# Zero products ahead of the first projection, the first weight tile between the halves of x, and one multiply from POOL to DVE

## The chip, the core and the metric

The kernel runs on one core of one Trainium2 chip. The core has five engines with a queue of instructions each: PE (TensorE, the matrix products; a product is a load of the stationary operand, shown as PEld, and a matmul), DVE (VectorE), ACT (ScalarE), POOL (GpSimd) and SP, which here only starts transfers. The metric is the device time of one execution in microseconds, the median of several runs. Beside it stands a profile of one execution: every instruction with its start, its duration and what ended the idle time of its engine before it. Times in the profile count from the first instruction.

## The reference

One layer of a streaming encoder, for x of 1024 tokens by 1024 channels, in float32. Three sub-layers, each normalised before and after and added to x:

```
h    = rms_norm(x, mix_pre_g);  proj = h @ w_in          # u, q, k, v, f_logit
y    = concat(rms_norm(s5_mixer(u)), rms_norm(forgetting_attention(q, k, v, f_logit)))
x    = x + rms_norm(y @ w_out)
x    = x + rms_norm(memory_cross_attention(rms_norm(x), rms_norm(mem)))
x    = x + rms_norm(swiglu(rms_norm(x), w_gate, w_up, w_down))
```

The parts that matter here are the very first product, u = h @ w_in[:, :512], and the very last steps: the down product of the SwiGLU, its norm with the gain `ffn_post_g`, and the addition of x.

## The kernel before

Every float32 product is made of three products of split operands. `split` (L112) makes the high part of an operand on ACT (a copy into a rounded type, L113, scaled by a gain where one is given) and the low part on DVE (the source less the high part, L115, or L117 with a gain). `mm3` (L121) then does high by high (L122), high by low (L123) and low by high (L124) into one bank of PSUM.

**The front.** The traced program begins with small constants and the first step of the generator `ssm()`, which prepares the tables of the state-space branch on DVE. Then, at a raised priority (L913), comes the projection of u. It runs over eight tiles k of 128 channels. For each k, x's transposed tile of 128x1024 is fetched (`x_fetch`, L201) and split with the gain `g_mix` (`x_split`, L207); the weight tile of 128x512 is fetched and split (`u_load`, L260); and `u_part` (L267) does 24 products, three for each of eight blocks of 128 tokens, into eight banks of 512 columns that add up over k. The first four banks come from the pool `g`, the other four are halves of two tiles of the pool `s`. For k = 0, x is fetched and split in two halves of 512 columns, and both are traced ahead of the weight. `x_square` (L212) adds up the squares of x on ACT and DVE for the norm; the norm's factor is applied to u afterwards (`u_scale`, L281).

Weights wait in two `raw` buffers and their split parts in three `whl` buffers, so a later weight can be split only when PE is done with an earlier one. After the last k, `u_keep` (L271) empties the banks; the state-space work then goes on, on DVE for the most part, between the other projections (`in_proj`, L885), the attention heads (`fox`, L705), the cross-attention and the SwiGLU.

**The end.** The down product is put together from seven groups of products. `take` (L1481) treats each bank as it comes. In the last group (n = 4) for each of four blocks j of 128 tokens it adds the bank to a kept sum on DVE (L1479), squares the result on ACT with a sum along the row (`square`, L1468) and multiplies it with the gain on POOL (L1476), in place, so the multiply waits for the square. `finish` (L1505) turns the two sums of squares into the factor r (`rsqrt_mean`, L126: L135 to L145 on DVE, L137 and L138 on ACT), and L1514 multiplies by r and adds x for each half row. For the last block, (t, j) = (1, 3), each half is stored as soon as it is done (L1517).

**What sets the order.** The program is traced in the order in which the Python runs. A planner then puts the instructions of each engine, and the transfers that SP starts, into a fixed order: it walks through a simulated time and takes among what is ready the instruction of the highest priority, the earlier traced one first (`schedule_with_timeline_sim=True`, L1603). On the chip each engine keeps that order and waits where an operand isn't there. A change in one place can therefore move instructions elsewhere.

Of the kernel before, what the change touches and what calls it, by code (L numbers as in the profile page):

```python
# [11 lines left out]
BF16 = mybir.dt.bfloat16  # L12
AF = mybir.ActivationFunctionType
ALU = mybir.AluOpType
# [3 lines left out]
P = 128  # L18
# [21 lines left out]
HID = ("11", "12", "22", "S1", "S2", "S3", "S4")  # L40
EVB = 13
OPB = 10


def bc(ap, axis, n):
# [7 lines left out]
def layer(ctx: ExitStack, tc: tile.TileContext, a, out):  # L53
    nc = tc.nc
    dve, act, pool, pe, sp = nc.vector, nc.scalar, nc.gpsimd, nc.tensor, nc.sync
# [13 lines left out]
    def slab(shape, dt=F32R):  # L69
        return slabp.tile(shape, dt, name="slab", tag="slab")  # L70

    def whl(shape, dt=F32R):
        return whlp.tile(shape, dt, name="whl", tag="whl")

    def raw(shape):
        return rawp.tile(shape, F32, name="raw", tag="raw")

    def g_ps(shape):
        return psg.tile(shape, F32, name="g", tag="g")

    def s_ps(shape):
        return pss.tile(shape, F32, name="s", tag="s")
# [20 lines left out]
    g_mix, g_xa, g_mem, g_out, g_pre_ffn = (gains[:, i, :] for i in range(5))  # L103
# [8 lines left out]
    def split(hi, lo, src, mul=None, lo_eng=None):  # L112
        first = act.activation(out=hi, in_=src, func=AF.Copy, scale=1.0 if mul is None else mul)  # L113
        if mul is None:
            (lo_eng or dve).tensor_tensor(out=lo, in0=src, in1=hi.bitcast(F32), op=ALU.subtract)  # L115
        else:
            dve.scalar_tensor_tensor(out=lo, in0=src, scalar=mul, in1=hi.bitcast(F32),  # L117
                                     op0=ALU.mult, op1=ALU.subtract)
        return first
# [75 lines left out]
    def tt(tag, shape=None, dt=F32):  # L195
        return t4.tile(shape or [P, S], dt, name=tag, tag=tag, bufs=BUFS[tag])
# [4 lines left out]
    def x_fetch(xts, k, n=1):  # L201
        x2t = slab([P, 2, S], F32) if k % 2 == 0 else xts[-1][0]
        xts.append((x2t, x2t[:, k % 2]))
        for cs in (slice(i * S // n, (i + 1) * S // n) for i in range(n)):
            sp.dma_start(out=xts[k][1][:, cs], in_=a["xT"][k * P:(k + 1) * P, cs])

    def x_split(xts, xs, k, n=1):  # L207
        for cs in (slice(i * S // n, (i + 1) * S // n) for i in range(n)):
            hi = split(xs[0][k][:, cs], xs[1][k][:, cs], xts[k][1][:, cs], g_mix[:, k:k + 1])
        return hi  # L210

    def x_square(xts, acc, k):  # L212
        if k == 0:
            act.activation(out=acc, in_=xts[k][1], func=AF.Square)
        else:
            sq = tt("b")
            act.activation(out=sq, in_=xts[k][1], func=AF.Square)
            dve.tensor_tensor(out=acc, in0=acc, in1=sq, op=ALU.add)
# [5 lines left out]
    def x_stats(acc):  # L224

        r = const.tile([P, L], F32, name="r_x")
        ps = s_ps([P, L])
        for j in range(L):
            pe.matmul(ps[:, j:j + 1], acc[:, j * P:(j + 1) * P], ones[:, 0:1], start=True, stop=True)
        rsqrt_mean(r, ps, D)  # L230
        return r, row_bcast(r, L)
# [28 lines left out]
    def u_load(k):  # L260
        w = raw([P, 512])
        sp.dma_start(out=w, in_=a["w_u"][k])
        hl = whl([P, 2, 512])
        split(hl[:, 0], hl[:, 1], w)
        return hl

    def u_part(banks, k, w, xh, xl):  # L267
        for j, ps in enumerate(banks):
            mm3(ps, xh[:, j * P:(j + 1) * P], xl[:, j * P:(j + 1) * P], w[:, 0], w[:, 1], k == 0, k == KT - 1)

    def u_keep(us, banks):  # L271

        for j, ps in enumerate(banks):
            p = ps.rearrange("c (g i) -> c g i", i=16)
            act.activation(out=us[0][:, :, L - 1 - j], in_=p[:, 0:16], func=AF.Copy)
            done = dve.tensor_copy(us[1][:, :, L - 1 - j], p[:, 16:32])
            if j == 3:
                last = done
        return us, last

    def u_scale(us, r):  # L281
        for j in range(L):
            a_, b_ = (u[:, :, L - 1 - j] for u in us)
            act.activation(out=a_, in_=a_, func=AF.Copy, scale=r[:, j:j + 1])
            dve.tensor_scalar(out=b_, in0=b_, scalar1=r[:, j:j + 1], scalar2=None, op0=ALU.mult)

    def qk_tile(i, xH, xL, rb, ahead=False):
        o = tt("a")

        def evac(h, hs, ps):  # L290
            dve.scalar_tensor_tensor(out=by_chunk(o)[:, 4 * h:4 * h + 4], in0=ps.rearrange("p (j c) -> p j c", j=4),
                                     scalar=-0.125 if i < 4 else 1.0,
                                     in1=rb[0][:, hs].rearrange("p (j c) -> p j c", j=4), op0=ALU.mult, op1=ALU.mult)
        yield from proj_tile(load_w(a["w_f"][i], P), xH, xL, evac, ahead)
        stA.dma_start(out=qk_d[i], in_=o)
# [572 lines left out]
    def step(g, n=1):  # L868
        for _ in range(n):
            if next(g, "end") == "end":  # L870
                return
# [40 lines left out]
    step(gs)  # L912
    with tc.high_priority(offset=boost):  # L913
        xts = []
        x_fetch(xts, 0, 2)
        xs = [[slab([P, 2, S]) for _ in range(KT // 2)] for _ in range(2)]
        xH, xL = ([x[k // 2][:, k % 2] for k in range(KT)] for x in xs)
        acc_x = tt("d")
        banks = [g_ps([P, 512]) for _ in range(4)]
        banks += [b[:, h * 512:h * 512 + 512] for b in (s_ps([P, S]) for _ in range(2)) for h in range(2)]  # L920
        ws = [u_load(0)]
        x_split(xts, (xH, xL), 0, 2)
        u_part(banks, 0, ws[0], xH[0], xL[0])
        for k in range(1, KT):
            x_fetch(xts, k)
            ws.append(u_load(k))
            x_split(xts, (xH, xL), k)
            u_part(banks, k, ws[k], xH[k], xL[k])
            x_square(xts, acc_x, k - 1)
        x_square(xts, acc_x, KT - 1)  # L930
        us = [slab([P, 16, L, 16], F32) for _ in range(2)]
        for t in us:
            dve.memset(t[:, 0, 0, 0:1], 0.0)
        u_c, kept = u_keep(us, banks)
        step(gs)
        with tc.issue_after(kept.ins):
            step(gs, 2)
        rb = []
        k4 = qk_tile(4, xH, xL, rb, ahead=True)
        step(k4)  # L940
        r_x, row = x_stats(acc_x)
        rb.append(row)
        u_scale(u_c, r_x)
# [91 lines left out]
    for j in range(NT):  # L1035
# [3 lines left out]
        t = tt("aab"[j % 3])  # L1039
# [3 lines left out]
        for h in range(2):  # L1043
            hs = slice(h * 512, h * 512 + 512)
# [26 lines left out]
    xT, xr, pts, x1_read = {}, {}, {}, []  # L1071
# [290 lines left out]
    tile_pool = lambda name, bufs: fst.enter_context(tc.tile_pool(name=name, bufs=bufs, reuse_waits="tile"))  # L1362
    evp, ssp, opp, wtp = (tile_pool("evp", EVB), tile_pool("ssp", 3), tile_pool("opp", OPB), tile_pool("wtp", 1))
    hid, made = {}, [None]
# [82 lines left out]
    g_fq = gp_.tile([P, D], F32, name="g_fq")  # L1447
# [18 lines left out]
    LO, HI = slice(0, 512), slice(512, 1024)  # L1466

    def square(t, j, h, src):  # L1468
        sq = bp.tile([P, 512], F32, name="sq", tag="sq")
        act.activation(out=sq, in_=src, func=AF.Square, accum_out=ssq[:, t, j, h:h + 1])  # L1470

    def quarter(t, j, hs):

        c = acc[t][j][:, hs]
        square(t, j, 0 if hs is LO else 1, c)
        pool.tensor_tensor(out=c, in0=c, in1=g_fq[:, hs], op=ALU.mult)  # L1476

    def add(o, ps, t):
        dve.tensor_tensor(out=o, in0=ps, in1=t, op=ALU.add)  # L1479
# [1 line left out]
    def take(n, j, ps):  # L1481

        e, o = acc[0][j], acc[1][j]
        if n == 1:
            act.activation(out=e[:, HI], in_=ps, func=AF.Copy)
        elif n == 6:
            add(o[:, LO], ps, e[:, HI])
        elif n == 2:
            square(0, j, 0, ps)
            dve.tensor_tensor(out=e[:, LO], in0=ps, in1=g_fq[:, LO], op=ALU.mult)  # L1490
        elif n == 5:
            add(e[:, HI], ps, e[:, HI])
        elif n == 7:
            add(o[:, HI], ps, e[:, HI])
            quarter(1, j, HI)
        elif n == 3:
            add(e[:, HI], ps, e[:, HI])
            quarter(0, j, HI)
            finish(0, j)
        else:  # L1500
            add(o[:, LO], ps, o[:, LO])
            quarter(1, j, LO)
            finish(1, j)
# [20 lines left out]
    banks = {}  # L1524
# [82 lines left out]
```

## Time and profile before

| | |
|---|---|
| time, median of 3 runs (lowest to highest) | 1432.68 us (1431.65 to 1433.4) |
| span of the profiled execution | 1428.8 us |
| profiled execution's own time | not given; the median is 3.9 us above the span |
| mean granted TensorE clock | 0.992 |
| busy: PE, PEld, DVE, ACT, POOL | 1390.7, 1187.5, 1003.7, 708.0, 410.9 us |
| HBM read, written | 168.90 MB, 76.81 MB |

A line of the timeline reads: start in us, duration in us, engine, line of the code, operation, output<-inputs by the program's names, shape, and in brackets the idle time of the engine just before it and what ended that. Neighbours alike are merged, with their count behind an x; a few per cent of the matmul records can be missing. "SPq" is SP's queue, where a line is the start of a transfer and not the transfer. A line of the windows view reads: the stretch, its length, the busy time and count of PE, PEld, DVE, ACT and POOL, the granted clock, the share of the DMA engines in use, and GB/s. A line of the groups reads: busy time in us, mean ns of one, then the idle time before them. A line of the view of one code line reads: the count, then the shortest, median and longest duration in ns. PE's matmuls are pipelined, so how fast they run is seen from the distance of their starts and not from their durations.

### The profile page before, as it was taken

The numbers are of one execution on the slowest core, as the hardware profiler recorded it, in microseconds if no ns is written. First come the engines' busy times: TensorE is split into PE (matmuls) and PEld (weight loads), VectorE is DVE, ScalarE is ACT, GpSimd is POOL, SyncE is SP. The second block draws the span as 40 slices with busy tenths as digits, with TensorE's granted clock in tenths as the row PEclk, the third lists the DMA queues.
The fourth block names the chain that finished last, engine by engine and source line by source line (L and its number), as shares of the span: only waits on it lengthen the run. The fifth ranks groups of instructions, "written<-read, shape, count | busy, mean of one in ns | idle before, by whom it ended". The sixth has DMA issues, their size and how long they took to land.

```text
span 1428.8 us, 20846 instructions
## 1 busy us (share of the span) xinstructions
PE 1390.7 (97%) x7422; PEld 1187.5 (83%) x7422; DVE 1003.7 (70%) x1818; ACT 708.0 (50%) x1421; POOL 410.9 (29%) x432
## 2 busy tenths in 40 slices
PE   7999999999999898999999999999999999999997
PEld 6889898889989886788888788888888888888886
DVE  7839947877888876645557677887766676565565
ACT  6373347777888754543434533333333334444341
POOL 0001000022243134001111367676666661000021
PEclk9999999999999999999999999999999999999999
DMA  6325654165654658323637455454444446965444
GB/s 204 98 80 148 183 192 132 33 204 178 193 153 120 172 164 276 134 74 109 193 112 236 149 190 173 168 181 154 164 156 162 162 155 227 334 219 192 177 162 162
DMA packets 112824, 238.43 MB, mean 167 GB/s; under 512 B 11848, under 2 KB 48712, under 8 KB 112592
## 3 DMA queue, kind: packets, MB, share of 16 engines
q1 hardware_dynamic: 96576, 182.01, 39.8%
q0 software_dynamic: 16144, 55.09, 10.6%
q8 instruction: 58, 0.95, 0.3%
q14 instruction: 46, 0.38, 0.1%
HBM read 168.90 MB, written 76.81 MB: 172 GB/s over the span
## 4 chain that ended last, share of the span: by engine, by line
PE 58%; DVE 1%; DMA 1%; ACT 0%; issue 0%; DVEq 0%; SPq 0%; ACTq 0%
PE x L1277 17%; PE g L1277 13%; PE x L1535 7%; PE g L1535 7%; PE x L123 2%; PE x L124 2%; PE x L122 2%; PE g L122 2%; PE g L124 2%; PE g L123 2%; PE g L1065 1%; DMA a<-t_d 1%; PE g L1173 1%; DVE slab L115 0%; DVE whl L115 0%; DVE c L1056 0%
## 5 line engine op out<-in xcount | busy, mean ns | idle before, releaser
L1277 PE MATMUL x<-slab,op 128*128 128x512 f32 x984 | 233.3, 389 | 0.5 <-DVE op L115 0.5
L1277 PEld LDWEIGHTS x<-slab,op 128*128 128x128 f32 x984 | 184.6, 188 | 39.3 <-DVE op L115 1.0
L1277 PE MATMUL g<-slab,op 128*128 128x512 f32 x744 | 178.7, 389 | 0.0
L115 DVE TENSOR_TENSOR slab<-slab 128x1024 fp32r<-128x1024 f32 (+2 forms) x92 | 110.2, 1207 | 84.7 <-ACT slab L113 82.8
L1277 PEld LDWEIGHTS g<-slab,op 128*128 128x128 f32 x744 | 139.6, 188 | 29.0
L122 PE MATMUL g<-slab,whl 128*128 128x512 f32 (+1 forms) x416 | 151.7, 365 | 0.6 <-ACT whl L113 0.4
L123 PE MATMUL g<-slab,whl 128*128 128x512 f32 (+1 forms) x416 | 148.4, 357 | 0.0
L124 PE MATMUL g<-slab,whl 128*128 128x512 f32 (+1 forms) x416 | 148.2, 357 | 0.0
L113 ACT ACTIVATE slab<-slab 128x1024 fp32r<-128x1024 f32 (+2 forms) x92 | 94.8, 1037 | 106.4 <-DMA slab<-hs_d 81.5
L1535 PE MATMUL g<-slab 128*128 128x512 f32 x462 | 126.6, 389 | 0.0
L1535 PE MATMUL x<-slab 128*128 128x512 f32 x462 | 126.6, 389 | 0.0
L1535 PEld LDWEIGHTS g<-slab 128*128 128x128 f32 x462 | 86.7, 188 | 18.0
L1535 PEld LDWEIGHTS x<-slab 128*128 128x128 f32 x462 | 86.7, 188 | 18.0
L122 PE MATMUL g<-whl,slab 128*128 128x256 f32 (+2 forms) x288 | 87.5, 309 | 9.6 <-ACT whl L113 7.3
L115 DVE TENSOR_TENSOR op<-slab,op 128x512 fp32r<-128x512 f32 x80 | 83.9, 1059 | 11.6 <-ACT op L113 11.3
L1353 POOL TENSOR_TENSOR wt<-wt 128x256 f32<-128x256 f32 x88 | 84.2, 957 | 19.9 <-DMA wt<-in_w_down 16.3
L113 ACT ACTIVATE op<-slab 128x512 fp32r<-128x512 f32 x80 | 50.0, 627 | 77.7 <-PE x L1277 37.5
L122 PEld LDWEIGHTS g<-slab,whl 128*128 128x128 f32 x416 | 78.6, 189 | 11.8 <-ACT whl L113 0.6
L124 PEld LDWEIGHTS g<-slab,whl 128*128 128x128 f32 x416 | 78.4, 189 | 11.6 <-DVE whl L115 0.2
L115 DVE TENSOR_TENSOR whl<-raw,whl 128x1024 fp32r<-128x1024 f32 (+2 forms) x61 | 72.0, 1184 | 22.3 <-ACT whl L113 21.7
L123 PEld LDWEIGHTS g<-slab,whl 128*128 128x128 f32 x416 | 78.6, 189 | 10.6
L123 PE MATMUL g<-whl,slab 128*128 128x256 f32 (+2 forms) x288 | 86.1, 299 | 0.0
(394 smaller groups left out, 3149.3 us busy)
## 6 DMA issues: line engine op xcount, KB each, us to landing
hs_d<-ev POOLq DMA_DIRECT2D x77, 256.0 KB, 2.6
slab<-hs_d SPq DMA_DIRECT2D x35, 512.0 KB
wt<-in_w_down SPq DMA_DIRECT2D x44, 256.0 KB
wt_d<-wt POOLq DMA_DIRECT2D x22, 512.0 KB, 4.8
slab<-in_w_gate SPq DMA_DIRECT2D x20, 512.0 KB
slab<-in_w_up SPq DMA_DIRECT2D x20, 512.0 KB
slab<-wt_d SPq DMA_DIRECT2D x20, 512.0 KB
wd_d<-in_w_down SPq DMA_DIRECT2D x33, 256.0 KB
```

The costliest lines, as they stand in the source:

```text
L113: first = act.activation(out=hi, in_=src, func=AF.Copy, scale=1.0 if mul is None else mul)
L115: (lo_eng or dve).tensor_tensor(out=lo, in0=src, in1=hi.bitcast(F32), op=ALU.subtract)
L122: pe.matmul(ps, lh, rh, start=first, stop=False)
L123: pe.matmul(ps, lh, rl, start=False, stop=False)
L124: pe.matmul(ps, ll, rh, start=False, stop=last)
L1065: pe.transpose(tp[:, k], src[:, (k0 + k) * P:(k0 + k + 1) * P], ident)
L1173: turned = pe.transpose(tp[:, k], h3[:, (4 * n + k) * P:(4 * n + k + 1) * P], ident)
L1277: pe.matmul(ps, x[:, k], y[:, k], start=first and k + n == 0, stop=k == 3 and n == 2, skip_group_check=not first)
L1353: pool.tensor_tensor(out=o, in0=x, in1=y, op=ALU.subtract)
L1535: pe.matmul(banks[n][j], xo[:, u, js], wo[:, v], start=ends[0] and k == 0, stop=ends[1] and k == 2, skip_group_check=onto is not None)
```

## The change

Four things. The first tile of x is no longer fetched and split as a whole ahead of the weight: a new function `x_half` fetches and splits one half, and the first weight tile is fetched and split between the two. (`x_fetch` with n = 0 now only reserves the buffer.) A bf16 tile of 128x512 is set to zero on DVE, and eleven products of it with itself are put on PE ahead of the first half of x; they write into the first bank, which the first real product starts afresh. They are no part of the result. With the weight's split traced ahead of the second half, it also stands ahead of the square of x's first tile. And in `quarter`, the multiply by the gain goes to DVE for the low half of the last block alone; the other eleven stay on POOL.

```diff
+WARM = 11
...
         xts = []
-        x_fetch(xts, 0, 2)
+        x_fetch(xts, 0, 0)
...
         acc_x = tt("d")
+
+        def x_half(i):
+            cs = slice(i * 512, i * 512 + 512)
+            sp.dma_start(out=xts[0][1][:, cs], in_=a["xT"][0:P, cs])
+            return split(xH[0][:, cs], xL[0][:, cs], xts[0][1][:, cs], g_mix[:, 0:1])
+
...
+        still = tt("yt", [P, 512], BF16)
+        dve.memset(still, 0.0)
+        for _ in range(WARM):
+            pe.matmul(banks[0], still[:, 0:P], still, start=True, stop=True)
+        x_half(0)
         ws = [u_load(0)]
-        x_split(xts, (xH, xL), 0, 2)
+        x_half(1)
         u_part(banks, 0, ws[0], xH[0], xL[0])
...
         square(t, j, 0 if hs is LO else 1, c)
-        pool.tensor_tensor(out=c, in0=c, in1=g_fq[:, hs], op=ALU.mult)
+        eng = dve if (t, j) == (1, 3) and hs is LO else pool
+        eng.tensor_tensor(out=c, in0=c, in1=g_fq[:, hs], op=ALU.mult)
```

## The prediction

> **What bounds the kernel now.** I read the page first, then the totals of PE's waits, then the timeline of the first 30 us engine by engine, then windows over the middle, and last the timeline of the end.
>
> ```profile
> span 1428.8 us, 20846 instructions
> ...
> PE 1390.7 (97%) x7422; PEld 1187.5 (83%) x7422; DVE 1003.7 (70%) x1818; ACT 708.0 (50%) x1421; POOL 410.9 (29%) x432
> ```
>
> PE is busy 97% of the span: 38.1 us of 1428.8 are not PE's. An edit pays if it removes PE time, PE waiting, or what stands after PE's last product. The totals of PE's waits, longest first (waited for: us in all, times, longest):
>
> ```profile
> PE g L122 <- ACT whl L113: 7.7, 2, 7.3
> PE x L122 <- DVE a L1048: 3.7, 4, 1.4
> ```
>
> The one long wait is the start: PE's first product waits 7.3 us for the high half of the first weight tile (`whl`, L113 on ACT). The next in the list is 3.7 us, and that in four pieces. Now PE's first products in its timeline (start, us, engine, line):
>
> ```profile
> 7.30 2.07 PE L122 MATMUL g<-whl,slab 128*128 128x512 f32 x4 [7.30 <-ACT whl L113]
> ...
> 10.02 0.63 PE L123 MATMUL g<-whl,slab 128*128 128x512 f32 x1
> ...
> 10.45 0.63 PE L124 MATMUL g<-whl,slab 128*128 128x512 f32 x1
> ...
> 13.01 0.43 PE L124 MATMUL g<-whl,slab 128*128 128x512 f32 x1
> 13.28 0.40 PE L123 MATMUL s<-whl,slab 128*128 128x512 f32 x1
> ...
> 15.55 1.07 PE L122 MATMUL g<-whl,slab 128*128 128x512 f32 x4
> ...
> 20.99 1.07 PE L122 MATMUL g<-whl,slab 128*128 128x512 f32 x4
> ```
>
> The 24 products of k=0 take 15.55 - 7.30 = 8.25 us; the 24 of k=1 take 20.99 - 15.55 = 5.44 us, 0.227 each. At 10.02 and 10.45 the starts are 0.43 apart, at 13.01 and 13.28 already 0.27. So PE runs at about half rate from 7.30 to 13.0, 5.7 us from its first product, and at full rate after that. The start thus costs 7.30 us of waiting and 2.8 us of slow products. The windows view writes the granted clock as 1.00 there all the same, so I go by the spacing:
>
> ```profile
> 7.30:8.50 1.20, 1.20 (x3) 1.01 (x4) 0.96 (x2) 0.00 (x0) 0.00 (x0) 1.00 0.99 344
> ```
>
> **The change part by part: the first weight tile between the halves of x.** These are ACT's first instructions and two of SP's issues:
>
> ```profile
> 4.09 0.72 ACT L113 ACTIVATE slab<-slab,gains 128x512 fp32r<-128x512 f32 x1 [2.08 <-DMA slab<-in_xT]
> ...
> 5.06 0.72 ACT L113 ACTIVATE slab<-slab,gains 128x512 fp32r<-128x512 f32 x1 [0.24 <-DMA slab<-in_xT]
> 5.69 1.04 ACT L214 ACTIVATE d<-slab 128x1024 f32<-128x1024 f32 x1
> ...
> 6.63 0.61 ACT L113 ACTIVATE whl<-raw 128x512 fp32r<-128x512 f32 x1
> ```
> ```profile
> 1.20 0.89 SPq L205 DMA_DIRECT2D slab<-in_xT  x2
> 2.13 0.43 SPq L262 DMA_DIRECT2D raw<-in_w_u  x1
> ```
>
> ACT waits for the two halves of x, which land just before 4.09 and 5.06, then squares all of x's first tile (1.04 us) and only then splits the weight at 6.63. Both halves and the weight tile are 128x512 f32, issued one after the other. The change swaps the second and third: the weight takes the second landing, about 5.0, and the second half of x the third. The third landing isn't shown; it lies between 5.06 and 6.63, one more step of 0.97 puts it at 6.0. ACT then splits the weight at 5.06 to 5.67, and PE's first product (first half of x, high parts) can start at about 5.75. The square moves behind the second half and waits for nobody PE needs. No other DMA is moved: the next issues (x tile 1, weight 1) keep their places on SP.
>
> **Products of a zero tile.** A memset of 128x512 bf16 on DVE, then 11 products on PE ahead of the first real one. The nearest row for the memset is one of 128x512 f32 at 485 ns; the tile has half the bytes, so 0.1 to 0.5 us. DVE's first instructions are these:
>
> ```profile
> 0.81 0.06 DVE L92 MEMSET ones<- 128x1 f32 x1 [0.81 <-PEq L1599]
> ...
> 1.45 0.43 DVE L90 CAST identb<-ident 128x128 bf16<-128x128 f32 x1 [0.52 <-POOL ident masks.py:199]
> ```
> ```profile
> L580 DVE MEMSET c<- 128x512 f32 x1 | 0.5, 485 | 0.1
> ```
>
> The memset's raised priority should put it first, at 0.81, so PE starts at about 1.2; behind the cast, which ends at 1.88, it would be 2.4. At 0.427 each (seven steps from 10.02 to 13.01) eleven products last 4.7 us: PE is free at 5.9, at worst 7.1. I take 5.9, just after the weight is ready. They write `banks[0]`, which the first real product starts afresh on the same engine, so no other engine waits on them. What they buy is the clock: if it rises 5.7 us after the first product as before, that is at 6.9, and only (6.9 - 5.9)/0.427 = 2.3 real products run slow, 0.5 us in excess. So k=0 ends at 5.9 + 5.44 + 0.5 = 11.8 instead of 15.55: 3.7 us. With 7.1 for PE and 8.1 for the clock it is 2.5 us; with PE at 5.75 and no slow product, 4.4 us.
>
> The Trainium skill's page TensorE: Matmul & The Clock Gate (Part 1: The HAM clock gate) puts the array at half clock until one free-running window of about 3.4 us has been busy throughout. By that the rise comes between 3.4 and 6.8 us after the first product; the 5.7 us of this trace lies inside, and by the page alone the gain of k=0 would be anything from about 3.2 to 4.4 us.
>
> **What is late next.** After k=0 PE needs the low parts of weights 1 and 2, made on DVE:
>
> ```profile
> 12.25 0.68 DVE L115 TENSOR_TENSOR whl<-raw,whl 128x512 fp32r<-128x512 f32 x1
> ...
> 17.91 0.68 DVE L115 TENSOR_TENSOR whl<-raw,whl 128x512 fp32r<-128x512 f32 x1
> ...
> 21.56 0.68 DVE L115 TENSOR_TENSOR whl<-raw,whl 128x512 fp32r<-128x512 f32 x1
> ```
>
> They end at 12.93, 18.59 and 22.24 and are fed by transfers, not by PE, so I leave them in place. PE begins k=1 at 11.8, does four high products (0.91) and needs the first at 12.7: waits 0.2. It begins k=2 at 17.4, needs the second at 18.4: waits 0.2. For k=3 it arrives at 23.1 with the third long done; later weights wait for one of three `whl` buffers that PE frees, so they move with PE. The front's gain is 3.7 - 0.4 = 3.3 us.
>
> Does it last? The stages behind are chains that PE itself feeds. The tight one is SSM work on DVE from 110 to 190:
>
> ```profile
> 60.00:70.00 10.00, 10.00 (x54) 8.54 (x53) 10.00 (x9) 2.13 (x6) 0.00 (x0) 1.00 0.02 4
> ...
> 90.00:100.00 10.00, 10.00 (x71) 9.14 (x69) 3.50 (x5) 8.54 (x22) 0.00 (x0) 1.00 0.00 0
> ...
> 140.00:150.00 10.00, 10.00 (x76) 7.95 (x76) 10.00 (x25) 4.24 (x9) 1.62 (x3) 1.00 1.04 263
> ...
> 190.00:200.00 10.00, 9.02 (x77) 8.63 (x76) 1.95 (x4) 4.63 (x9) 1.62 (x3) 1.00 0.94 287
> ```
>
> DVE (third busy column) is full at 60 and again at 140, but only 3.50 of 10 at 90, so it can start the tight stretch earlier with PE. PE loses 0.98 us where it meets the end of it at 190. I carry the 3.3 through.
>
> **The last scaling multiply on DVE.** The end, after PE's last product:
>
> ```profile
> 1420.80 0.63 ACT L1470 ACTIVATE sq<-acc 128x512 f32<-128x512 f32 x1 [6.20 <-DVE acc L1479]
> ...
> 1421.55 0.21 DVE L139 TENSOR_SCALAR rsv<-ssq,rse 128x1 f32<-128x1 f32 x1 [0.79 <-ACT sq L1470]
> 1421.60 1.26 POOL L1476 TENSOR_TENSOR acc<-acc,g_fq 128x512 f32<-128x512 f32 x1 [6.18 <-ACT sq L1470]
> 1421.88 0.20 ACT L138 ACTIVATE rsy<-rsy 128x1 f32<-128x1 f32 x1
> 1422.12 0.76 DVE L141 SCALAR_TENSOR_TENSOR rst<-rsy,rsv 128x1 f32<-128x1 f32 x1 [0.35 <-ACT rsy L138]
> 1422.91 0.16 DVE L145 SCALAR_TENSOR_TENSOR r<-rst,rsy 128x1 f32<-128x1 f32 x1
> 1423.10 1.42 DVE L1514 SCALAR_TENSOR_TENSOR x<-acc,r,x 128x512 f32<-128x512 f32 x2
> ```
> ```profile
> L141 DVE SCALAR_TENSOR_TENSOR rst<-rsy,rsv x40: 200/218/1259, 527.2 to 1422.1; 128x1 f32<-128x1 f32 x40
> ```
> ```profile
> L1490 DVE TENSOR_TENSOR acc<-g,g_fq x2: 692/692/692, 1299.1 to 1300.5; 128x512 f32<-128x512 f32 x2
> ```
>
> POOL's multiply ends at 1422.86, and L141, one element per partition, lasts until 1422.88 although its median is 218 ns. It sat out the multiply. On DVE the multiply costs 0.69 (L1490, the same shape), starts at 1421.6 and ends at 1422.3; L139 goes beside it in the queue, L141 (0.2), L145 (0.16) follow, and L1514 starts at 1422.7 instead of 1423.10: 0.4 us. Queued behind the multiply on DVE are just these, and only the last store waits for them. Bounds: nothing, if the multiply starts 0.4 late, to 0.5.
>
> The Trainium skill's page SBUF — State Buffer (Who interferes with whom) says that a DVE instruction with two SBUF inputs and a GpSimd instruction that reads SBUF exclude each other for the whole instruction. The 0.76 us of L141, over with POOL's multiply, agrees.
>
> Sum: 3.3 + 0.4 = 3.7 us. The profiled span goes from 1428.8 to 1425.1. The median of the runs, 1432.68, is 3.9 above that span (the profiled execution's own time isn't given), and I take that rest as unchanged: 1432.68 - 3.7 = 1429.0.
>
> **The rivals.** First, zero products don't raise the clock, because the array does no work on zeros. Nothing in the trace shows a product of zeros. Then only the earlier start counts: 7.30 - 5.9 = 1.4, less nothing further on, plus 0.4: 1432.68 - 1.8 = 1430.9. Chance 0.08.
>
> Second, the front's gain is absorbed: DVE's full stretches, fixed by their own work, hold PE at 190 for the 3.3 us that it comes earlier. For it speak the full 10.00 at 60 and 140, against it the idle 6.5 of 10 at 90. The end's 0.4 stays: 1432.3. Chance 0.16.
>
> Third, slower. Line 1603 has the planner order every engine by a simulated time; with a front that differs, it can queue a weight split behind blocks of SSM work on DVE, with PE waiting. These are the sizes:
>
> ```profile
> 44.76 1.23 DVE L115 TENSOR_TENSOR whl<-raw,whl 128x1024 fp32r<-128x1024 f32 x1 [1.29 <-ACT whl L113]
> ...
> 54.32 2.28 DVE L449 TENSOR_TENSOR slab<-c 128x2048 f32<-128x2048 f32 x1
> ```
> ```profile
> 53.63 0.39 PE L122 MATMUL g<-slab,whl 128*128 128x512 f32 x1
> ```
>
> A block is 2.28 us. The split that ends at 45.99 is used at 53.63, with 7.6 us to spare, four blocks at least; against it, then. Once the spare is gone each block costs PE 2.28; one leaves a gain, two (4.56) eat it, three (6.84) give 1432.68 - 3.7 + 6.84 = 1435.8. Chance 0.13.
>
> **How the numbers follow.** The measurement can tell about 0.2%, 2.9 us, from no change: faster is below 1429.8, slower above 1435.5. My forecast has 0.58 and spans 2.5 + 0 to 4.4 + 0.5, that is 1427.8 to 1430.2; a twentieth of it falls short of 2.9. A re-planned order that saves a further block of 2.28 beyond it has the remaining 0.05 (1426.7). Faster: 0.55 + 0.05 = 0.60. Same: 0.03 + 0.08 + 0.16 = 0.27. Slower: 0.13. The range reaches from 1426.7 over the forecast, both rivals that gain less, to 1433.6, half a block above the absorbed case; the slower rival and a little beside it stay out.
>
> **What would show it.** Right: eleven bf16 products from about 1.2 to 5.9 us on PE; the first L122 at 5.8 to 6.1; products at 0.227 from about 7; k=1 beginning near 11.8 and k=2 near 17.4; PE's later waits as before; L1476 on DVE at 0.69, L141 near 0.2, and L1514 0.4 us nearer to the last product. Wrong: products at 0.43 after 9 us (zeros don't count); a first L122 after 7; new waits of PE on `whl` or `slab` from DVE in the first 200 us that sum to more than 1 us; or PE's waits in the middle, from 190 to 590, grown by over 2 us.

## The result, and the profile after

| | before | after |
|---|---|---|
| median of 5 runs (lowest to highest) | 1431.65 us (1431.34 to 1433.4) | 1425.97 us (1425.94 to 1426.95) |
| ratio, 95% interval | | 0.996 (0.9948 to 0.9972) |
| span of the profiled execution | 1428.8 us | 1424.8 us |
| profiled execution's own time | not given | 1426.61 us |

The change gains 4.0 to 7.4 us by the interval of the ratio; the prediction had 3.7. Its time, 1429.0, is 3.0 above the measured median, and the lower end of its range, 1426.7, is 0.7 above it. In the two profiles the difference of the spans is 4.0. New line numbers: up to about line 916 each line has moved down by one, by 12 after that, and by 13 behind the multiply in `quarter` (its L1476 is now L1489, L1514 is L1527; `mm3`'s three products are L123 to L125).

The page after, its span and its totals:

```profile
span 1424.8 us, 20868 instructions
...
PE 1393.3 (98%) x7433; PEld 1187.9 (83%) x7433; DVE 1002.8 (70%) x1820; ACT 708.4 (50%) x1421; POOL 410.9 (29%) x431
```

PE is busy for 2.6 us more, with eleven more products, in a span that is 4.0 shorter. The waiting has shrunk, and the 7.7 us for `whl` at the head of PE's waits is gone. The list after is headed by another one, which comes back below:

```profile
PE g L783 <- ACT slab L114: 4.7, 1, 4.7
```

**The front.** The timeline after, first 18 us (start, duration, engine, line; PEld is the weight load that goes ahead of each matmul):

```profile
0.86 0.27 DVE L929 MEMSET yt<- 128x256 uint32 x1 [0.86 <-PEq L1612]
...
1.19 3.89 PE L931 MATMUL g<-yt 128*128 128x512 bf16 x11 [1.19 <-DVE epsc L96]
...
3.30 0.15 PEld L931 LDWEIGHTS <-yt 128*128 128x128 bf16 x1 [0.28 <-issue]
3.73 0.15 PEld L931 LDWEIGHTS <-yt 128*128 128x128 bf16 x1 [0.28 <-issue]
4.06 0.53 PEld L931 LDWEIGHTS <-yt 128*128 128x128 bf16 x3 [0.18 <-issue]
4.63 0.63 ACT L114 ACTIVATE whl<-raw 128x512 fp32r<-128x512 f32 x1
5.31 1.20 PE L123 MATMUL g<-whl,slab 128*128 128x512 f32 x4 [0.23 <-ACT whl L114]
6.74 0.72 ACT L114 ACTIVATE slab<-slab,gains 128x512 fp32r<-128x512 f32 x1 [1.47 <-DMA slab<-in_xT]
...
10.97 1.20 PE L123 MATMUL g<-whl,slab 128*128 128x512 f32 x4
11.82 0.68 DVE L116 TENSOR_TENSOR whl<-raw,whl 128x512 fp32r<-128x512 f32 x1
12.56 0.50 PE L124 MATMUL g<-whl,slab 128*128 128x512 f32 x1
...
16.79 1.07 PE L123 MATMUL g<-whl,slab 128*128 128x512 f32 x4
```

The weight loads of the zero products stand 0.43 apart up to 3.73, then 0.33 and less: the clock goes full between 3.73 and 4.06, 2.5 to 2.9 us after the first of them. The first real product starts at 5.31 at full rate. k=0 ends at 10.97 instead of 15.55, k=1 at 16.79 instead of 20.99: 4.20 us ahead. The difference between the two steps, 0.38, is PE's waiting for the first low part (it ends at 12.50, and L124 starts at 12.56). In k=2 PE waits a little for the next low part too (0.09 in all), so at the start of k=3 (26.43 before, 22.32 after) the lead is 4.11.

**The loss between 60 and 95 us.** The timeline before, then the one after:

```profile
68.92 2.28 DVE L455 TENSOR_TENSOR slab<-slab 128x2048 f32<-128x2048 f32 x1
...
71.66 0.17 DVE L145 SCALAR_TENSOR_TENSOR r_x<-rst,rsy 128x8 f32<-128x8 f32 x1
...
71.86 3.31 ACT L284 ACTIVATE slab<-slab,r_x 128x256 f32<-128x256 f32 x8 [3.43 <-DVE r_x L145]
...
76.27 1.09 ACT L175 ACTIVATE d<-s 128x512 f32<-128x512 f32 x2 [1.10 <-PE s L172]
...
95.28 0.47 PE L122 MATMUL g<-slab,whl 128*128 128x512 f32 x1
```
```profile
67.99 2.28 DVE L456 TENSOR_TENSOR slab<-slab 128x2048 f32<-128x2048 f32 x1
...
70.38 0.17 DVE L146 SCALAR_TENSOR_TENSOR r_x<-rst,rsy 128x8 f32<-128x8 f32 x1
...
70.58 3.30 ACT L285 ACTIVATE slab<-slab,r_x 128x256 f32<-128x256 f32 x8 [7.53 <-DVE r_x L146]
...
74.86 1.05 ACT L176 ACTIVATE d<-s 128x512 f32<-128x512 f32 x2
...
75.97 1.20 PE L464 MATMUL s<-ident,slab 128*128 128x128 f32 x8 [1.28 <-ACT d L176]
...
80.11 0.66 PE L476 MATMUL g<-ident,slab 128*128 128x128 f32 x4 [0.29 <-DVE a L292]
...
92.62 0.48 PE L123 MATMUL g<-slab,whl 128*128 128x512 f32 x1
```

PE comes some 4 us earlier, but DVE, full here, finishes its 2.28-us blocks only 0.9 us earlier. Behind them stands `r_x`, the norm's factor. ACT waits 7.53 us for it instead of 3.43, spends 3.30 on `u_scale`, and only then copies the row of factors out of PSUM (L176), 1.41 earlier than before. PE, whose next work needs the bank that this copy empties, waits 1.28 and later 0.29. At 92.62 against 95.28 the lead is 2.66: of 4.20 us, 1.54 are lost on the way to there.

From there the lead doesn't stay as it is: it is 4.66 at 478 us (the first product after a wait of 2.30 us for L117 on DVE, L118 after the change), and 2.67 at the end. That this is the 2.66 of 95 us again is chance, as the table under e7 and e8 shows. Last addition of a bank, before and after:

```profile
1420.07 0.69 DVE L1479 TENSOR_TENSOR acc<-x,acc 128x512 f32<-128x512 f32 x1 [3.00 <-PE x L1535]
```
```profile
1417.40 0.69 DVE L1492 TENSOR_TENSOR acc<-x,acc 128x512 f32<-128x512 f32 x1 [3.00 <-PE x L1548]
...
1418.88 0.69 DVE L1489 TENSOR_TENSOR acc<-acc,g_fq 128x512 f32<-128x512 f32 x1 [0.79 <-ACT sq L1482]
...
1419.49 0.21 DVE L140 TENSOR_SCALAR rsv<-ssq,rse 128x1 f32<-128x1 f32 x1
1419.80 0.22 DVE L142 SCALAR_TENSOR_TENSOR rst<-rsy,rsv 128x1 f32<-128x1 f32 x1
...
1420.25 1.41 DVE L1527 SCALAR_TENSOR_TENSOR x<-acc,r,x 128x512 f32<-128x512 f32 x2
```

The difference is 2.67. **The tail**: from there to the last two multiplies it took 1423.10 - 1420.07 = 3.03 before and takes 2.85 now, a gain of 0.18. L142 is down from 0.76 to 0.22 without POOL beside it, but L140, which before ran beside POOL's multiply, now stands behind DVE's. A second gain comes after that: from the start of these two to the end of the span it was 5.70 and is 4.55, with the same stores. The view of the end barrier's line, POOL's row of it, before and after (count, then shortest, median and longest in ns, first and last start):

```profile
L1603 POOLq DRAIN  x3: 40/93/6457, 1421.6 to 1428.5; - x3
```
```profile
L1616 POOLq DRAIN  x3: 40/102/6486, 1411.4 to 1424.5; - x3
```

POOL closes with a DRAIN, an instruction of the end barrier, of about 6.5 us; it is the longest of the three and the first to start, and it starts with POOL's last multiply. Before, that was at 1421.6, so it ended at 1428.1, and the span ended 0.7 later. Now POOL's last multiply is one block of tokens earlier, and the DRAIN is over at 1417.9. Now SP, which waits for the store, is later than POOL (SP's first DRAIN stands at 1423.9).

Sum of the profiles: 2.67 + 0.18 + 1.15 = 4.0, the whole difference of the spans.

### The profile page after: what moved, and what is told of

It is laid out like the page before. It is cut to its first block, busy times and chain, and to the rows that moved or that the text cites. A ratio compares the mean times of both kernels' runs of the same rounds, so it can differ in the third digit from the quotient of the medians.

```text
span 1424.8 us, 20868 instructions
## 1 busy us (share of the span) xinstructions
PE 1393.3 (98%) x7433; PEld 1187.9 (83%) x7433; DVE 1002.8 (70%) x1820; ACT 708.4 (50%) x1421; POOL 410.9 (29%) x431
## 4 chain that ended last, share of the span: by engine, by line
PE 59%; DVE 1%; DMA 1%; ACT 0%; issue 0%; DVEq 0%; SPq 0%; ACTq 0%
PE x L1289 17%; PE g L1289 13%; PE x L1548 7%; PE g L1548 7%; PE x L124 2%; PE x L125 2%; PE g L123 2%; PE x L123 2%; PE g L125 2%; PE g L124 2%; PE g L1077 1%; DMA a<-t_d 1%; PE g L1185 1%; DVE c L1068 0%; DVE whl L116 0%
## 5 line engine op out<-in xcount | busy, mean ns | idle before, releaser
L123 PE MATMUL g<-slab,whl 128*128 128x512 f32 (+1 forms) x416 | 151.7, 365 | 0.4 <-ACT whl L114 0.4
L125 PE MATMUL g<-slab,whl 128*128 128x512 f32 (+1 forms) x416 | 148.4, 358 | 0.0
L124 PE MATMUL g<-slab,whl 128*128 128x512 f32 (+1 forms) x416 | 148.3, 356 | 0.0
L123 PEld LDWEIGHTS g<-slab,whl 128*128 128x128 f32 x416 | 78.6, 189 | 11.6 <-ACT whl L114 0.6
L123 PE MATMUL g<-whl,slab 128*128 128x256 f32 (+2 forms) x288 | 85.7, 306 | 2.6 <-DVE sv_f L240 1.8
L125 PEld LDWEIGHTS g<-slab,whl 128*128 128x128 f32 x416 | 78.4, 189 | 11.7 <-DVE whl L116 0.2
L124 PEld LDWEIGHTS g<-slab,whl 128*128 128x128 f32 x416 | 78.7, 189 | 10.6
L124 PE MATMUL g<-whl,slab 128*128 128x256 f32 (+2 forms) x288 | 85.4, 296 | 0.0
```

What stands on the lines that cost most here:

```text
L123: pe.matmul(ps, lh, rh, start=first, stop=False)
L124: pe.matmul(ps, lh, rl, start=False, stop=False)
L125: pe.matmul(ps, ll, rh, start=False, stop=last)
```

## The experiments

Theory: the front brings PE 4 us, of which the late row of factors takes a third; the tail brings 0.2 on DVE and 1.15 at POOL's DRAIN. Rivals: the parts don't add up because the planner's other order makes or loses the time; the end got shorter by chance. Beside e1 to e4 the kernel before took 1430.29 us in the median (1425.43 to 1433.44, 35 runs).

**e1_tail_only: only the multiply on DVE.** The changed kernel with zero products and the new load order taken back:

```diff
-        still = tt("yt", [P, 512], BF16)
-        dve.memset(still, 0.0)
-        for _ in range(WARM):
-            pe.matmul(banks[0], still[:, 0:P], still, start=True, stop=True)
         x_half(0)
-        ws = [u_load(0)]
         x_half(1)
+        ws = [u_load(0)]
```

> Only the last scaling multiply moves to DVE; the front is that of before. Theory of the prediction: the step from the last square to L1514's first product shortens by about 0.4 us (the changed kernel's trace has 0.18), so the time falls by 0.2 to 0.4 us, inside the uncertainty. Rival (the end holds the missing gain, because the last store's landing also gets shorter): the time falls by 1.3 us or more and the stretch from the last store's issue to the end of the span is about 2.8 us instead of 3.9.

Measured: 1429.85 us (1425.51 to 1435.21, 12 runs), ratio 0.9999 (0.9987 to 1.0011). The median doesn't show a gain, and an interval of 1.7 us to each side can't exclude the 1.3. Its profile has it: the last two multiplies start 2.85 us after the last addition, as in the changed kernel, and 4.52 before the end, where the kernel before has 5.70:

```profile
1419.73 0.69 DVE L1492 TENSOR_TENSOR acc<-x,acc 128x512 f32<-128x512 f32 x1 [3.00 <-PE x L1548]
...
1422.58 1.42 DVE L1527 SCALAR_TENSOR_TENSOR x<-acc,r,x 128x512 f32<-128x512 f32 x2
```

**e2_front_only: all but the multiply.**

```diff
-        eng = dve if (t, j) == (1, 3) and hs is LO else pool
+        eng = pool
```

> The zero products and the new order of the first loads, with the last multiply on POOL as before. Theory (the front carries nearly all): 5.0 to 5.5 us below before, with PE 4.1 us ahead at k=3 and the rest found later on. Rival (the end carries more than a microsecond): 4.4 us or less below before.

Measured: 1426.61 us (1425.62 to 1429.21, 12 runs), ratio 0.9977 (0.9968 to 0.9986), 2.0 to 4.6 us. The front alone makes most of the difference, but less than the 5.0 to 5.5 that were expected.

**e3_order_only: the weight between the halves, no zero products, POOL's multiply** (e2's edit and the first four removed lines of e1's).

> No zero products; only the first weight tile between the halves of x. Theory (the clock is a part of its own): the first product starts at about 5.3 us, but runs at half rate until a clock rise 2.8 to 5.7 us later, so PE is about 2 us less ahead at k=2 than in the changed kernel (2 instead of 4.2), and the time is 2 to 3.5 us below before. Rival (zero products buy nothing, only the earlier start counts): as fast as front only.

Measured: 1429.91 us (1427.53 to 1432.26, 12 runs), ratio 1.0001 (0.9991 to 1.0011): not the 2 to 3.5 us that were expected.

**e4_warm_only: the zero products, the old order of loads, POOL's multiply** (e2's edit and the last two changed lines of e1's).

> Only the eleven zero products; the loads in the order of before. Theory: the clock is up at about 4 us, the first product still waits until 7.3 us and runs at full rate, k=0 takes about 5.5 instead of 8.25 us, and PE is 2.5 us ahead at k=2; if the clock falls back in the idle stretch between the zero products (over at 5.1) and 7.3, less. Time 2 to 3.5 us below before. Rival (the earlier load is what counts): within 1 us of before.

Measured: 1430.38 us (1426.11 to 1433.3, 12 runs), ratio 1.0001 (0.9989 to 1.0012). The first real products and the start of k=1, timelines of e3 and of e4:

```profile
5.51 2.07 PE L123 MATMUL g<-whl,slab 128*128 128x512 f32 x4 [5.51 <-ACT whl L114]
...
13.80 1.07 PE L123 MATMUL g<-whl,slab 128*128 128x512 f32 x4
```
```profile
1.19 4.38 PE L931 MATMUL g<-yt 128*128 128x512 bf16 x11 [1.19 <-DVE yt L929]
...
7.16 1.19 PE L123 MATMUL g<-whl,slab 128*128 128x512 f32 x4 [1.59 <-ACT whl L114]
...
12.75 1.07 PE L123 MATMUL g<-whl,slab 128*128 128x512 f32 x4
```

With the order alone PE starts 1.79 us earlier and runs its first four products in 2.07, at half clock; it begins k=1 1.75 ahead of before (15.55). With the zero products alone it starts as late as before, but at full clock, and begins k=1 2.80 ahead. 1.75 + 2.80 = 4.55, and both together have 4.58. At the product that stands at 95.28 before, e3 is 0.74 ahead (94.54), e4 1.78 (93.50), e2 2.58 (92.70): both lose about 1.0 on the way. So up to 95 us the parts add up in the profiles. Behind that they don't: at the last addition (1420.07 before) e3 is 0.62 us behind the kernel before, and e4 2.59 ahead. Nor do they in the times: the medians of e3 and e4 show no gain (their intervals reach 1.3 and 1.6 us), while e2, with both parts, lies 3.3 below e3 and 3.8 below e4. Neither part shows a gain by itself, so the rival that the order further on makes or loses the time stands. For e4, whose profiled execution was among its fastest (1427.96), the miss stays open.

**e5_after_again: the changed kernel once more.** No edit; beside it, e6 and e7 the kernel before took 1429.61 us (1427.6 to 1433.8, 17 runs).

> The changed kernel once more, with more executions of both kernels. Theory (the change is worth what the two profiles show, 2.7 us at PE's end, 0.2 ahead of the last store and 1.15 behind it, 4.0 in all; the rest of the first comparison's 5.7 is the scatter of single executions, which spans 8 us for before): the median is 3 to 5 us below that of before. Rival (a re-planned order brings 1.7 us more that the one profile hides): 5 us or more below.

Measured: 1427.06 us (1424.65 to 1429.62, 12 runs), ratio 0.9978 (0.9968 to 0.9988): 1.7 to 4.6 us. Of the 4.0 to 7.4 of the first comparison only the lower end is borne out; 4.0, the difference of the spans, lies inside this interval and at the edge of the first.

**e6_pool_last: a small copy on POOL that waits for the last square.** It writes a tile that nobody reads.

```diff
         eng.tensor_tensor(out=c, in0=c, in1=g_fq[:, hs], op=ALU.mult)
+        if eng is dve:
+            pool.tensor_copy(sm(1, "late"), ssq[:, t, j, 0:1])
```

> The changed kernel with one more POOL instruction at the end, a copy of one element per partition that waits for the last square, as the multiply did. Theory (POOL's closing drain lasts about 6.5 us from its last instruction on, whatever that is, and was the last to end): the end of the span moves back to about 6.5 us after the last square, so from the start of L1527's last pair of steps to the end of the span it is 5.6 to 5.8 us instead of 4.5. Rival (the drain is long because the multiply is): 4.5 us as in the changed kernel.

Measured: 1428.98 us in one run, span 1427.1. Its timeline and the row of the end barrier:

```profile
1420.47 0.70 POOL L1491 COPY late<-ssq 128x1 f32<-128x1 f32 x1 [6.17 <-ACT sq L1482]
...
1421.81 1.42 DVE L1529 SCALAR_TENSOR_TENSOR x<-acc,r,x 128x512 f32<-128x512 f32 x2
```
```profile
L1618 POOLq DRAIN  x3: 40/102/5882, 1420.5 to 1426.9; - x3
```

The last multiplies start 5.29 us before the end, against 4.55 without the copy and 5.70 with the whole multiply on POOL. The DRAIN starts with the copy and ends at 1426.4, 0.7 before the end, as before. It lasts 5.88 for a copy of 0.70 and 6.46 for a multiply of 1.26: about 5.2 us beyond the instruction in both. So POOL's DRAIN does set the end, and the gain isn't chance. It is less than expected (5.6 to 5.8) because the DRAIN's length goes with POOL's last instruction, and the copy is the shorter one.

**e7_stats_first and e8_stats_again: the factor of the norm at a raised priority.** If DVE's late `r_x` is what takes 1.5 us, the planner should put it ahead of the SSM blocks:

```diff
-        r_x, row = x_stats(acc_x)
+        with tc.high_priority(offset=boost):
+            r_x, row = x_stats(acc_x)
```

> The changed kernel with the norm of x (x_stats) at a further raised priority, so that its five short DVE steps come ahead of the 2.28 us blocks of SSM work. Theory (PE loses 1.4 of the 4.1 us between 60 and 80 us because the norm's factor stands behind those blocks on DVE, and the copy of its row behind u_scale on ACT): the wait of 1.28 us for the row at 76 us goes, and PE is 3.5 to 4 us ahead of before at the first L486 instead of 2.6; the time is about 1 us below the changed kernel. Rival (the stretch is bound by the blocks themselves): PE still 2.6 us ahead there, the time that of the changed kernel.

Measured: 1423.58 us (1421.87 to 1424.76, 6 runs), ratio to before 0.9953 (0.9937 to 0.9969), and 3.5 below e5, where 1 was expected. The timeline of e7:

```profile
66.39 0.15 DVE L146 SCALAR_TENSOR_TENSOR r_x<-rst,rsy 128x8 f32<-128x8 f32 x1
...
66.58 3.31 ACT L285 ACTIVATE slab<-slab,r_x 128x256 f32<-128x256 f32 x8 [3.14 <-DVE r_x L146]
...
71.19 1.09 ACT L176 ACTIVATE d<-s 128x512 f32<-128x512 f32 x2 [1.29 <-PE s L173]
...
87.21 0.47 PE L486 MATMUL g<-slab 128*128 128x128 f32 x2
```

`r_x` is there 4.0 us earlier than after the change, L176 waits for PE again, as before the change, and PE's wait of 1.28 us is gone. At the first product of L486 (91.70 before) the lead is 4.49: so far the front's gain is whole.

> The changed kernel with the statistics of x at a raised priority, as in the run before, repeated beside more runs of the kernel before. Theory (the front's 4.1 us, cut to 2.7 by the late row of x at 60 to 80 us, can be kept whole): the median is 4.5 to 7.0 us below the kernel before of the same call, and 1.5 to 4.5 below the 3.2 by which the changed kernel's own repeat lay under it. Rival (the first 7 us were luck of one set of executions): 2.5 to 4.0 below, like the changed kernel.

Measured: 1424.51 us (1422.0 to 1425.52, 6 runs) beside 1432.33 (1427.6 to 1433.3, 11 runs), ratio 0.9951 (0.9937 to 0.9966): 4.9 to 9.0 us. It held, and the rival that the first result was luck falls. This version beats both kernels.

Its gain over the changed kernel, 3.5 us, is more than the 1.8 that it has kept at 90 us. The profiles show where the rest comes from. How far PE is ahead of the kernel before, in us, at the same four instructions (they start at 15.55, 95.28, 478.46 and 1420.07 before):

| profile | k=1 | 95 us | 478 us | last addition |
|---|---|---|---|---|
| after | 4.58 | 2.66 | 4.66 | 2.67 |
| e5 (the changed kernel) | 4.33 | 3.10 | 3.93 | 2.34 |
| e6 (the changed kernel and a copy) | 4.45 | 3.43 | 3.07 | 1.11 |
| e2 (changed front) | 4.19 | 2.58 | 3.45 | 1.54 |
| e7 | 4.44 | 4.50 | 4.81 | 5.33 |
| e8 (e7's kernel) | 4.43 | 4.75 | 5.00 | 5.98 |

At 478 us the changed kernel has, in one execution, all of its first lead back; in the others it is 0.4 to 1.4 us short of it. Between 478 us and the end it loses 1.6 to 2.0 us, where e7's kernel gains 0.5 to 1.0. The place is near 500 us. Timelines after the change and of e7:

```profile
497.99 1.06 ACT L114 ACTIVATE slab<-raw 128x1024 fp32r<-128x1024 f32 x1 [7.57 <-DMA raw<-in_w_out_f]
...
499.59 0.58 PE L783 MATMUL g<-slab 128*128 128x256 f32 x1 [4.71 <-ACT slab L114]
```
```profile
495.42 1.06 ACT L114 ACTIVATE slab<-raw 128x1024 fp32r<-128x1024 f32 x1 [4.46 <-DMA raw<-in_w_out_f]
...
497.01 0.39 PE L783 MATMUL g<-slab 128*128 128x256 f32 x1 [1.60 <-ACT slab L114]
```

ACT's next instruction splits a tile of output weights that is still being fetched, and the split that PE needs stands behind it in ACT's queue. PE's wait, which heads the list after the change, is that of ACT, less the work that PE still has. Behind it the granted clock is lower. The windows view (granted clock in the third column from the right) has, after the change and in e7:

```profile
500.00:510.00 10.00, 10.00 (x43) 8.69 (x43) 5.76 (x7) 4.13 (x7) 0.80 (x1) 0.71 0.50 159
```
```profile
500.00:510.00 10.00, 9.58 (x60) 8.40 (x59) 5.17 (x7) 4.77 (x7) 0.79 (x1) 1.00 0.57 177
```

With PE all but full in both, 43 products were done there at a granted clock of 0.71, and 60 at 1.00. This goes with the kernel and not with the execution: PE's wait is 4.71 and 4.60 in the two profiles of the changed kernel, 5.11 in e6 and 3.82 in e2, but 1.60 and 1.45 in e7 and e8 (1.97 before). Whether the earlier `r_x` does it, by way of the order that follows from it, and why the weights come sooner there, isn't shown. So e7 and e8 show that the factor's place costs PE up to 1.8 us by 95 us, and that this kernel is faster; that the second follows from the first is only argued.

**e9_fill: e7's kernel with 20 products of the identity ahead of two groups of products.** Executions of one kernel lie up to 8 us apart (1425.4 to 1433.4 for the kernel before). The idea was that stretches of low clock, which come behind PE's waits, lie at other places in other executions; the experiment was to keep PE busy where it waits.

```diff
             yp = g_ps([P, 256])
+            if h == NH - 1 and qc >= 2:
+                for _ in range(20):
+                    pe.matmul(yp[:, 0:P], identb, identb, start=True, stop=True)
```

> The same kernel and 20 more products of the 128x128 identity with itself on PE ahead of the products of values with the probabilities, for the last head and its last two blocks of queries (about 475 to 510 us); they write a bank that the first real product starts afresh. Theory A (executions differ because PE idles there for some us and the granted clock then falls for 3.4 or 6.8 us at a place that varies): the stretches of half clock between 470 and 510 us go, highest and lowest time come closer (spread under 2.5 us, where the run beside it has 3 to 5), and the median is 0 to 3 us lower. Rival B (the scatter has other sources): the spread stays as it is, and the median is 0 to 2 us higher, by the products themselves where they aren't hidden.

Measured: 1425.55 us (1423.75 to 1429.33, 6 runs), ratio 0.9961 (0.9946 to 0.9977); the spread is 5.6 us beside e8's 3.5. Its timeline, and the windows view of one stretch:

```profile
481.97 0.36 PE L786 MATMUL g<-slab 128*128 128x256 f32 x1 [1.79 <-DVE slab L116]
...
496.88 1.29 PE L781 MATMUL g<-identb 128*128 128x128 bf16 x20
...
500.72 0.39 PE L786 MATMUL g<-slab 128*128 128x256 f32 x1 [1.54 <-ACT slab L114]
```
```profile
482.90:486.40 3.50, 3.50 (x20) 3.43 (x19) 3.07 (x6) 2.58 (x6) 0.43 (x1) 0.51 0.59 158
```

The planner put the fillers at 488.8 and 496.9, where PE had work, and PE's waits of 1.79 and 1.54 stayed; half clock follows the first of them. The waits weren't filled, so this says nothing on theory A. Against the idea itself speak the pairs of profiles of one kernel: from 460 to 520 us the mean granted clock is 0.91 in both of the changed kernel and 0.97 in both of e7's kernel, and only a stretch between 270 and 290 us differs (0.91 in one profile of the changed kernel, 1.00 in the other). What makes executions differ stays open.

## Why the prediction was wrong, point by point

**The step that failed is the base**: "The median of the runs, 1432.68, is 3.9 above that span (the profiled execution's own time isn't given), and I take that rest as unchanged: 1432.68 - 3.7 = 1429.0." In every execution of this study for which both are known the time is 1.7 to 1.9 us above its span, not 3.9. By that the profiled execution before took about 1430.6 us (an estimate), and the median of three lay 2 us above it by scatter. Terms read from that profile belong to 1430.6: 1430.6 - 3.7 = 1426.9, and the profiled execution after took 1426.61. Of the 3.0 us by which the forecast was too high, 2.1 are this base, 0.3 the gain (4.0 in the spans for 3.7), and 0.6 is again scatter: the median after lies that far below the profiled execution. The range had the bounds of every cost in it, but no term for the scatter of the kernel itself: three runs, 1431.65 to 1433.4, looked as if it were small, and 35 runs reach from 1425.4 to 1433.4. Two of its bounds don't follow either: the gain of 4.4 + 0.5 leaves out PE's waits for the low parts, about 1 us with PE that early, and half a block above 1432.3 is 1433.4 and not 1433.6. Neither changes the outcome.

**Zero products**: right. They ran from 1.19 to 5.08 and raised the clock; the first rival (zeros don't count, 1430.9) is refuted by the weight loads' distances, and by e4. The clock rose earlier than forecast, 2.5 to 2.9 us after the first product where 5.7 was carried over from before, so no real product ran slow (0.5 us in the sum). Other executions were less quick: 3.0 to 3.3 us in e5, about 3.4 to 3.8 in e4 and e7, and in e2 all eleven ran at half rate. The Trainium skill's page TensorE: Matmul & The Clock Gate (Part 1: The HAM clock gate) asks for a busy window of about 3.4 us and has the moment vary by about 0.5 us from run to run. e4, e5 and e7 agree with that; the trace after the change, at 2.5 to 2.9 us, has it earlier, and the measurement decides.

**First weight tile**: right, and better than forecast. Its split starts at 4.63 where 5.06 was set, the first real product at 5.31 instead of 5.9. The second half of x lands later than forecast (6.74), and PE doesn't feel it. k=0 ended at 10.97, not 11.8: 4.58 instead of 3.7. The two waits for low parts, 0.4 in all, came as 0.38 in k=1 and 0.09 in k=2, so that 4.11 was left at k=3 where the sum had 3.3.

**"I carry the 3.3 through"**: half right. Of 4.20, 2.66 was there at 95 us, 4.66 at 478 us and 2.67 at the end. The second rival named DVE's full stretches as what absorbs the gain, but at 190 us and whole; it was in part, at 60 to 80 us, where the same 10.00 stood in the quoted window. The idle 6.5 of 10 at 90 doesn't help a factor that is queued at 70. e7 shows it: with `r_x` ahead of the blocks 4.49 arrives. The slower rival (a split of a weight behind SSM blocks) didn't come about, though its mechanism did with `r_x` in the split's place, at a price of 1.5. What holds the gain down at the end is another place, which the prediction named only as a sign of being wrong ("PE's waits in the middle, from 190 to 590, grown by over 2 us"): near 500 us PE's wait for a split on ACT grew from 1.97 to 4.71. The sum of the waits didn't grow (PE is busy for 379.5 of these 400 us before and 380.1 after).

**The tail**: the mechanism on DVE was right (0.69, L142 at 0.22; the Trainium skill's page SBUF — State Buffer, Who interferes with whom, has a DVE instruction with two SBUF inputs and a GpSimd one that reads SBUF shut each other out, and the 0.76 beside POOL's multiply agrees), but it gave 0.18 instead of 0.4, because "L139 goes beside it in the queue" was wrong: the multiply ended 2.17 us after the last addition (2.23 in the forecast), but L140, as L139 is called now, came behind it, so L142 started at 2.40, and L1527 at 2.85 instead of 2.6. Missing altogether was the closing DRAIN on POOL, which gave 1.15. So the tail was sized at 0.4 and measured 1.3.

In the sum 3.3 + 0.4 became 2.67 + 1.33: 4.0 instead of 3.7, with errors of -0.6 and +0.9 that nearly cancel. That the gain came out so near is luck, and so is the 2.67, which is 1.11 to 2.67 in the four profiles of the changed front.

**Left open**: why the parts of the front by themselves show no gain in the medians of twelve runs (e3's profile has lost its lead by the end, e4's has not); why the output weights near 500 us come later after the change than in e7; and what makes executions of one kernel differ.

## What to carry to other kernels

A profile's terms belong to the time of that one execution: set them against its span plus what lies around a span, and put the scatter of the kernel itself into the range. When PE comes earlier, look for small results (a norm's factor, a row of statistics) that stand on another engine behind long blocks; they keep their time, and the gain shrinks there unless they are moved ahead too. Follow the lead over the whole kernel before saying where a gain was lost: here it shrank at 70 us, came back by 478 us and went again near 500 us. At the end of a kernel look at every engine's last instruction, not only at those on the path to the last store.

## What the runs showed of the hardware

- POOL's DRAIN at the end of the program lasts until about 5.2 us after POOL's last instruction: 6.46 with a multiply of 1.26, 5.88 with a copy of 0.70. Where POOL's last instruction ended 5.9 us before the end of the span (before, e6), nothing but 0.7 us came after this DRAIN; where it ended 12 us before (after), SP was later.
- Products of zeros raise the granted clock: full rate 2.5 to 2.9 us after the first of them after the change, while in the kernel before it took 5.7 us from the first real product. The moment differs between executions: in e4 the weight loads of the zero products were still 0.43 apart up to 4.58, and in e2 up to the last at 5.01.
- The step L141 of the norm's factor on DVE, one element per partition, took 0.76 us when it started beside a POOL multiply of 128x512, and 0.22 without one (as L142 after the change). L139, started just before that multiply, took its usual 0.21.
